# Two down-product operands made in PSUM, and normalization factors kept there, in a one-layer decoder step on Trainium2

## The chip, the cores and the metric

The kernel runs on one core of a Trainium2 chip. The metric is the device time of one execution in microseconds (us): median 1795.73 us of 3 runs, 1795.71 to 1795.86. Five engines work side by side: PE (matmul), DVE (elementwise, VectorE), ACT (activation, copies, casts, ScalarE), POOL (elementwise, GpSimd) and SP, which issues the DMAs. Each runs its own instructions in a fixed order and waits where a value or a buffer is not ready. Matmul results go to PSUM, which this kernel cuts into eight banks. Everything else lies in SBUF.

## What is computed

One layer of a hybrid decoder on 16 meta, 1024 prompt and 32 sample tokens of width 1024, in f32:

```python
x = x + 0.5 * swiglu(rmsnorm(x, g1), w1g, w1u, w1d)
h = rmsnorm(x, gm)
z = h @ w_in + b_in
...
x = x + jnp.concatenate([c, q], axis=-1) @ w_out + b_out
x = x + 0.5 * swiglu(rmsnorm(x, g2), w2g, w2u, w2d)
...
y = xf * lax.rsqrt(jnp.mean(xf * xf, axis=-1, keepdims=True) + EPS)     # rmsnorm, then * g
return (jax.nn.silu(x @ wg) * (x @ wu)) @ wd                            # swiglu
```

The two lines left out make c (gated depthwise convolution) and q (pooling) from z. A last rmsnorm gives the outputs.

## The kernel before

**Tokens and numbers.** The 1072 tokens and 2 of padding are cut into three pieces of 358 columns. Feature tiles of 128 lie on the partitions, tokens on the free axis. Every f32 operand is split into a high part in fp32r and a low remainder (`split`: ACT casts the high part, DVE subtracts it to make the low part, L145), and each product is three matmuls (`mul`, L127). Weights come by DMA (`wraw`), ACT casts the high part `wh` (L144) and POOL subtracts for the low part `wl` (L145).

**The two fast passes.** Each FFN has 22 tiles of width, taken in 11 pairs. The first FFN runs a pass over pieces one and two, the second FFN one over two and three, as a block form with seven products instead of eight (`m1` to `m7`). DVE makes the sums of raw weight blocks (`block_steps`, L556 to L559) and, after the products, the sums in `settle` and `add` (L586). Products m3 to m7 stay in their PSUM banks until these sums are done. The result of a gate block goes through `gate`: ACT writes its silu into an SBUF buffer `cc` (L712 in a group, L684 in a plain pair) and the bank is free. The result of an up block goes through `up`.

**Groups.** Eight of the eleven pairs are joined two by two (`group_sink`, four groups in each pass), so that their down product runs in the seven-product form too (`fast_down`). It needs seven operands made of the hidden blocks: b11, b21, t1 to t4, b22. The second pair of a group makes most of them, for halves i = 1 and then i = 0, in this chain on DVE: the block product (L716) into `cc` for b21 and into its own bank for b22; t2 in the bank of b22 by L707 and L708; t3 by the same two lines into an SBUF buffer `tmp`; and t4 by L732 into `cc`. Each is then split (L144 on ACT, L145 on DVE: `dt4l`, `dt3l`). The operands b11, b21, t2 and part of t3 lie in borrowed tiles: `xb` and `hid0` to `hid2`. A down product takes two banks in turn, and DVE adds it to x (L634). While DVE makes these operands, PE already runs the gate block of the next pair and then the down products.

**Normalizations.** `rms_all` or `rms` squares and sums a piece, `rsqrt` (L187 on) takes the root in small DVE operations and lets PE spread the factor over the partitions of a bank. ACT copies it to SBUF as `nr` (L218). `normed` and `fast_operands` then form x times gain times factor (`scaled`, L266) with `x` and `nr` both in SBUF, and split it. Five normalizations run beside matmuls: h1b, hma (two pieces), h2a, s2 (`fast_operands`) and hmb. Plain passes (`plain_ffn`, L505 to L531) run beside them on PE. The first normalization has code of its own (class `Start`) and already reads its factor from the bank; the last one, of the outputs, calls `rms`. The change touches neither.

**Order.** Matmuls stay in program order. All other instructions are ordered by a tile scheduler that lays out a timeline of its own; it also decides which bank a tile gets. POOL has little but the low parts of weights, in the order of the weights.

Of the kernel before, what the change touches and what calls it, by code (L numbers as in the profile page):

```python
# [12 lines left out]
ALU = mybir.AluOpType  # L13
P = 128

D = 1024
# [15 lines left out]
EPS = 1e-6  # L32
# [53 lines left out]
def trunk(ctx: ExitStack, tc: tile.TileContext, xt, wf1, win, wout, wf2, wpool, vec, eye, sconv, spool,  # L86
          yt, ncp, npp, ncs, nps):
    nc = tc.nc
# [9 lines left out]
    def temp():  # L98
        return const.tile([P, N + PHIST - 1], F32, name="tmp", tag="tmp", bufs=T_BUFS)
# [21 lines left out]
    def accum():  # L121
        return pp.tile([P, 512], F32, name="acc", tag="acc")
# [119 lines left out]
    def rms(piece, out):  # L242
        s = yield from square_sum([X(k, piece) for k in range(KD)])
        yield LAG
        out[piece] = yield from rsqrt(s, 1.0 / D, EPS)
# [21 lines left out]

    def rms_all(pieces, out):

        steps, last = None, None  # L270
        for piece in pieces:
            s = yield from square_sum([X(k, piece) for k in range(KD)])
            if steps is not None:
                out[last] = whole(steps)
            yield LAG
            steps, last = rsqrt(s, 1.0 / D, EPS), piece
            next(steps)
        if steps is not None:
            yield LAG2
            out[last] = whole(steps)  # L280

    def normed(pieces, gain, tiles, out, stats=None):


        st = {} if stats is None else stats
        h, lo = tiles()
        yield from rms_all([piece for piece in pieces if piece not in st], st)
        at, lows = 0, []
        for piece in pieces:
            n = piece[1] - piece[0]  # L290
            for k in range(KD):
                t = accum()[:, :n]
                with tc.issue_after(lows[-2].ins) if len(lows) > 1 else nullcontext():
                    scaled(t, piece, k, gain, st[piece])
                yield
                lows.append(split(h[:, k, at : at + n], lo[:, k, at : at + n], t))
                yield
            at += n
        out["h"] = (h, lo)
# [7 lines left out]
    def fast_operands(pieces, gain, out, stats):  # L307

        st = stats
        p0, p1 = pieces
        n = p0[1] - p0[0]
        ops = out["ops"] = operand_tiles(n)

        def put(name, k, t):
            split(ops[name][0][:, k], ops[name][1][:, k], t)

        for piece in pieces:
            if piece not in st:  # L320
                yield from rms(piece, st)
        sub = nc.vector.tensor_tensor
        for k in range(KH):
            b11, b22, b21 = (temp()[:, :n] for _ in range(3))
            t = accum()[:, :n]
            scaled(b11, p0, k, gain, st[p0])
            scaled(b22, p1, KH + k, gain, st[p1])
            yield
            put("b11", k, b11)
            put("b22", k, b22)  # L330
            yield
            scaled(t, p1, k, gain, st[p1])
            t3 = temp()[:, :n]
            sub(t3, b22, t, ALU.subtract)
            sub(t, t, b11, ALU.subtract)
            yield
            put("t1", k, t)
            put("t3", k, t3)
            scaled(b21, p0, KH + k, gain, st[p0])
            yield  # L340
            sub(t, b22, t, ALU.subtract)
            put("t2", k, t)
            put("b21", k, b21)
            yield
            sub(t, b21, t, ALU.subtract)
            put("t4", k, t)
            yield LAG6
# [298 lines left out]
    def fast_ffn(wsrc, pieces, free, get, hid):  # L646

        n = N  # L650
        pairs, downs = [], {}

        def kept():
            return pools["fast"].tile([P, n], F32, name="cc", tag="cc", bufs=4)

        def own(name, part):
            return [pools["fast"].tile([P, n], F32R, name=f"d{name}{'hl'[part]}{i}", tag=f"d{name}{'hl'[part]}{i}")
                    for i in range(2)]

        def borrowed():  # L660

            t = const.tile([P, KD, n], F32R, name="xb", tag=f"x{free}")
            out = {name: tuple([t[:, 4 * i + 2 * part + j] for j in range(2)] for part in range(2))
                   for i, name in enumerate(("b11", "b21"))}
            out["t2"] = tuple([hidden_tile(i, part) for i in range(2)] for part in range(2))
            out["t3"] = ([hidden_tile(2, part) for part in range(2)], own("t3", 1))
            return out

        def places(p):

            for i in range(2):
                if p < PAIRS - 1:
                    hid[2 * p + i] = tuple(own(("t1", "t4")[i], part) for part in range(2))
                elif i == 0:
                    hid[2 * p + i] = tuple(own("b22", part) for part in range(2))
                else:
                    hid[2 * p + i] = tuple([hidden_tile(j, part) for j in (1, 2)] for part in range(2))

        def plain_sink(p):
            silus = {}  # L680

            def gate(i, c, t):
                silus[i, c] = kept()
                nc.scalar.activation(silus[i, c], t, AF.Silu)  # L684

            def up(i, c, t):
                f = 2 * p + i
                nc.vector.tensor_tensor(t, t, silus[i, c], ALU.mult)
                if f not in hid:
                    places(p)  # L690
                split(hid[f][0][c], hid[f][1][c], t)

            return gate, up

        def group_sink(ops, second):
            silus, hs = {}, {}
            sub = nc.vector.tensor_tensor

            def put(name, i, t):
                if not ops:  # L700
                    ops.update(borrowed())
                if name not in ops:
                    ops[name] = own(name, 0), own(name, 1)
                split(ops[name][0][i], ops[name][1][i], t)

            def less(t, s, name, i):
                sub(t, s, ops[name][0][i], ALU.subtract)  # L707
                sub(t, t, ops[name][1][i], ALU.subtract)  # L708

            def gate(i, c, t):  # L710
                silus[i, c] = kept()
                nc.scalar.activation(silus[i, c], t, AF.Silu)  # L712

            def up(i, c, t):
                h = hs[i, c] = t if c else silus[i, c]
                nc.vector.tensor_tensor(h, t, silus[i, c], ALU.mult)  # L716
                if second:
                    put("b22" if c else "b21", i, h)
                elif c == 0:
                    put("b11", i, h)  # L720
                if (i, 1 - c) not in hs:
                    return
                if not second:
                    sub(hs[i, 1], hs[i, 1], hs[i, 0], ALU.subtract)
                    put("t1", i, hs[i, 1])
                    return
                b21, b22, t3 = hs[i, 0], hs[i, 1], temp()[:, :n]
                less(b22, b22, "t1", i)
                put("t2", i, b22)
                less(t3, b22, "b11", i)  # L730
                put("t3", i, t3)
                sub(b21, b21, b22, ALU.subtract)  # L732
                put("t4", i, b21)

            return gate, up

        for p in range(PAIRS):
            start = p if p in GROUPS else p - 1
            if start in GROUPS:
                if p == start:  # L740
                    ops = {}
                    downs[p + 1] = [fast_down(wsrc, p, j, pieces, ops) for j in range(2)]
                gate, up = group_sink(ops, p != start)
            else:
                gate, up = plain_sink(p)
                downs[p] = down_steps(wsrc, p, pieces, hid)
            pairs.append((fast_pair(wsrc[4 * p], wsrc[4 * p + 1], get, n, gate),
                          fast_pair(wsrc[4 * p + 2], wsrc[4 * p + 3], get, n, up)))
        return pairs, downs, places
# [243 lines left out]
    def whole(gen):  # L993

        while True:
            try:
                next(gen)
            except StopIteration as e:
                return e.value
# [14 lines left out]
    box = {k: {} for k in ("s1", "h1b", "hma", "hmb", "ca", "cb", "h2a", "s2")}  # L1014
# [209 lines left out]
    last, room = {}, {}  # L1224
# [65 lines left out]
    steps = [p for p in plan if p[0] == "step"]  # L1290
# [22 lines left out]
    i = 0  # L1313
    credit = 0.0
    for item in plan:
# [3 lines left out]
        while state["made"] <= min(i + 2, len(steps) - 1):  # L1319
            s = steps[state["made"]]  # L1320
# [96 lines left out]
```

## Time and profile before

| | before |
|---|---|
| median of 3 runs | 1795.73 us (1795.71 to 1795.86) |
| the profiled execution | 1794.0 us |
| its span on the core | 1792.2 us |
| PE busy | 1726.9 us, 96% |
| DVE busy | 1384.0 us, 77% |
| POOL busy | 1146.5 us, 64% |
| ACT busy | 759.7 us, 42% |

The span is the time from the first to the last instruction that the profiler saw; the execution adds 1.8 us around it. Busy shares are averages over stages that differ, so they do not tell where PE waits. The views used below are the table of what PE waited for, the timeline (start, duration, engine, line, operation, and in brackets the idle time before it with what ended it) and the groups of DVE instructions by line and form.

### The profile page before, as it was taken

Reading aid. Unit: us, or ns where it says so; the run is one execution under the profiler, and the core shown is the slowest. Engines: PE = TensorE matmul, PEld = TensorE weight load, DVE = VectorE, ACT = ScalarE, POOL = GpSimd, SP = SyncE. Lnnn points to the kernel's source line nnn. Section 1 sums busy time; section 2 is a strip of 40 time slices with the busy share of each in tenths; the row PEclk is TensorE's granted clock in tenths of the full one; section 3 lists DMA queues with packets and bytes.
Section 4 is the critical chain, followed back from the end, with each engine's and each line's share of the span. In section 5 each row is a group of like instructions: output and inputs, shape, how many; then the busy total and the mean of one; then the engine's idle time right before and its main releaser. Section 6 shows DMA issues by size and latency. Waiting matters only on the chain.

```text
span 1792.2 us, 29876 instructions
## 1 busy us (share of the span) xinstructions
PE 1726.9 (96%) x10486; PEld 1710.3 (95%) x10486; DVE 1384.0 (77%) x2621; ACT 759.7 (42%) x1482; POOL 1146.5 (64%) x894
## 2 busy tenths in 40 slices
PE   7799999999999999999999999999999999999997
PEld 6799999999998999999999998999999999999997
DVE  8869898989657795897235888548588989897965
ACT  6434444444444224434235433455453444444344
POOL 5586666667745337667356657765577676767683
PEclk9899999999999999999999999999999999999998
DMA  6122232223353223443234494444332222222232
GB/s 210 33 82 76 71 104 76 70 81 104 101 115 110 81 67 116 124 134 108 71 100 136 130 137 128 136 125 128 108 110 88 71 83 71 83 71 71 71 101 84
DMA packets 115894, 177.70 MB, mean 99 GB/s; under 512 B 28321, under 2 KB 35745, under 8 KB 115745
## 3 DMA queue, kind: packets, MB, share of 16 engines
q1 hardware_dynamic: 115744, 175.80, 33.4%
q8 instruction: 83, 1.36, 0.3%
q14 instruction: 67, 0.54, 0.1%
HBM read 170.60 MB, written 5.15 MB: 98 GB/s over the span
## 4 chain that ended last, share of the span: by engine, by line
PE 73%; DVE 19%; issue 3%; DMA 2%; ACT 1%; POOL 1%; SPq 0%; DVEq 0%; POOLq 0%; ACTq 0%
PE acc L127 73%; DMA wraw<-in_wf 2%; DVE wraw L558 1%; DVE acc L586 1%; DVE tmp L586 1%; DVE acc L830 1%; DVE wraw L557 1%; DVE tmp L708 1%; DVE acc L266 1%; DVE tmp L266 1%; DVE x L505 1%; POOL wl L145 1%; DVE pr L848 1%; DMA x<-in_xt 0%; DVE cc L716 0%
## 5 line engine op out<-in xcount | busy, mean ns | idle before, releaser
L145 POOL TENSOR_TENSOR wl<-wraw,wh 128x512 fp32r<-128x512 f32 x740 | 992.5, 1353 | 581.1 <-ACT wh L144 539.3
L144 ACT CAST wh<-wraw 128x512 fp32r<-128x512 f32 x740 | 452.9, 621 | 662.7 <-PE acc L127 438.8
L127 PE MATMUL acc<-smt,wh 128*128 128x358 f32 x1024 | 253.0, 328 | 1.8 <-DVE mixl L145 1.8
L830 DVE SCALAR_TENSOR_TENSOR acc<-ub,vecs,acc 128x340 f32<-128x340 f32 (+2 forms) x348 | 183.3, 570 | 2.6
L127 PEld LDWEIGHTS acc<-smt,wh 128*128 128x128 f32 x1024 | 181.8, 190 | 2.5 <-DVE mixl L145 2.1
L127 PE MATMUL acc<-smt,wl 128*128 128x358 f32 x512 | 167.7, 328 | 0.0
L127 PE MATMUL acc<-mixlt,wh 128*128 128x340 f32 x704 | 166.7, 321 | 0.8 <-ACT wh L144 0.8
L505 DVE SCALAR_TENSOR_TENSOR x<-acc,x 128x358 f32<-128x358 f32 (+1 forms) x240 | 119.3, 516 | 35.6 <-PE acc L127 34.9
L634 DVE SCALAR_TENSOR_TENSOR x<-acc,x 128x358 f32<-128x358 f32 x320 | 144.8, 515 | 0.0
L586 DVE TENSOR_TENSOR acc<-tmp,acc 128x358 f32<-128x358 f32 x168 | 85.7, 526 | 49.4 <-PE acc L127 46.1
L127 PEld LDWEIGHTS acc<-mixlt,wh 128*128 128x128 f32 x704 | 122.1, 190 | 1.3 <-ACT wh L144 1.1
L127 PE MATMUL acc<-mixlt,wl 128*128 128x340 f32 x352 | 112.8, 320 | 0.8 <-POOL wl L145 0.8
L145 POOL TENSOR_TENSOR wl<-sx,wh 128x512 fp32r<-128x512 f32 x58 | 85.0, 1465 | 29.8 <-ACT wh L144 28.0
L127 PEld LDWEIGHTS acc<-smt,wl 128*128 128x128 f32 x512 | 97.0, 189 | 0.0
L558 DVE TENSOR_TENSOR wraw<-sx,wraw 128x512 f32<-128x512 f32 x58 | 78.6, 1355 | 13.5 <-POOL wl L145 13.4
L127 PE MATMUL acc<-mixh,wh 128*128 128x356 f32 (+1 forms) x320 | 78.4, 325 | 2.1 <-ACT mixh L144 2.1
L127 PE MATMUL acc<-mixl,wh 128*128 128x356 f32 (+1 forms) x320 | 78.0, 325 | 0.0
L127 PE MATMUL acc<-mixh,wl 128*128 128x356 f32 (+1 forms) x320 | 77.9, 325 | 0.0
L557 DVE TENSOR_TENSOR wraw<-wraw 128x512 f32<-128x512 f32 x58 | 75.8, 1307 | 0.4
L586 DVE TENSOR_TENSOR tmp<-tmp,acc 128x358 f32<-128x358 f32 x126 | 65.3, 518 | 14.0 <-PE acc L127 12.8
L559 DVE TENSOR_TENSOR wraw<-wraw 128x512 f32<-128x512 f32 x58 | 71.6, 1235 | 1.6 <-POOL wl L145 1.5
L127 PE MATMUL acc<-b11h,wh 128*128 128x358 f32 x184 | 62.1, 338 | 10.8 <-ACT wh L144 10.8
(286 smaller groups left out, 4765.8 us busy)
## 6 DMA issues: line engine op xcount, KB each, us to landing
wraw<-in_wf SPq DMA_DIRECT2D x544, 256.0 KB, 2.9
wraw<-in_win SPq DMA_DIRECT2D x48, 256.0 KB, 2.9
wraw<-in_wout SPq DMA_DIRECT2D x32, 256.0 KB, 2.9
x<-in_xt SPq DMA_DIRECT2D x8, 179.0 KB, 4.5
tmp<-in_xt SPq DMA_DIRECT2D x8, 179.0 KB, 2.8
x<-in_xt SPq DMA_DIRECT2D x1, 1432.0 KB, 7.3
x<-in_xt SPq DMA_DIRECT2D x8, 178.0 KB, 4.4
out_yt<-tmp SPq DMA_DIRECT2D x8, 170.0 KB, 3.3
```

The costliest lines, as they stand in the source:

```text
L127: tc.keep_in_program_order(nc.tensor.matmul(acc, lhs, rhs, start=start, stop=stop))
L144: nc.scalar.copy(hi, src)
L145: return (engine or nc.vector).tensor_tensor(lo, src, hi, ALU.subtract)
L266: nc.vector.scalar_tensor_tensor(t, X(k, piece), col(gain, k), r, ALU.mult, ALU.mult)
L505: nc.vector.scalar_tensor_tensor(X(m, piece), acc, 0.5, X(m, piece), ALU.mult, ALU.add)
L557: nc.vector.tensor_tensor(a21, a11, a21, ALU.subtract)
L558: nc.vector.tensor_tensor(a11, s1, a11, ALU.subtract)
L559: nc.vector.tensor_tensor(a12, a12, a11, ALU.subtract)
L586: nc.vector.tensor_tensor(t, s, acc, ALU.add)
L634: nc.vector.scalar_tensor_tensor(to, acc, 0.5 * sign, to, ALU.mult, ALU.add)
L708: sub(t, t, ops[name][1][i], ALU.subtract)
L830: nc.vector.scalar_tensor_tensor(to, src, w, part, ALU.mult, ALU.add)
```

## The change

Two edits. In a group's second pair, t4 is now made before t3. t3 is made in place in the bank of b22. For i = 1 the product b21 also stays in its bank, ACT copies it to SBUF as an operand, and t4 is made in the bank; for i = 0 it stays in `cc`. In the five normalizations the factors stay in their banks (`box["psum"]`) while `scaled` runs over all tiles; factors that are already known in SBUF (one for h1b, one for s2) are copied by ACT into a bank.

```diff
     def rms_all(pieces, out):
...
+        def done(piece, box):
+            whole(steps)
+            out[piece] = box["psum"]
...
             if steps is not None:
-                out[last] = whole(steps)
+                done(*last)
             yield LAG
-            steps, last = rsqrt(s, 1.0 / D, EPS), piece
+            box = {}
+            steps, last = rsqrt(s, 1.0 / D, EPS, box, False), (piece, box)
             next(steps)
...
+    def in_banks(pieces, st):
+
+        known = [piece for piece in pieces if piece in st]
+        yield from rms_all([piece for piece in pieces if piece not in st], st)
+        for piece in known:
+            r = accum()[:, : piece[1] - piece[0]]
+            nc.scalar.copy(r, st[piece])
+            st[piece] = r
+        yield
...
-        yield from rms_all([piece for piece in pieces if piece not in st], st)
+        yield from in_banks(pieces, st)
...
-        for piece in pieces:
-            if piece not in st:
-                yield from rms(piece, st)
+        yield from in_banks(pieces, st)
...
             def up(i, c, t):
-                h = hs[i, c] = t if c else silus[i, c]
+                h = hs[i, c] = t if c or (second and i) else silus[i, c]
...
-                b21, b22, t3 = hs[i, 0], hs[i, 1], temp()[:, :n]
-                less(b22, b22, "t1", i)
-                put("t2", i, b22)
-                less(t3, b22, "b11", i)
-                put("t3", i, t3)
-                sub(b21, b21, b22, ALU.subtract)
+                b21, t = hs[i, 0], hs[i, 1]
+                if i:
+                    t4 = temp()[:, :n]
+                    nc.scalar.copy(t4, b21)
+                less(t, t, "t1", i)
+                put("t2", i, t)
+                sub(b21, t4 if i else b21, t, ALU.subtract)
                 put("t4", i, b21)
+                less(t, t, "b11", i)
+                put("t3", i, t)
```

PE's order is the same as before, and so is POOL's but for one place in the sample tokens' part. What moves stands on DVE. The names carry the tile's number here; lines of the changed kernel are 15 or 16 higher (L707 is L722, L708 is L723, L732 is L748, L586 is L601). This is DVE at the end of the third group of the first pass (315 to 335 us of the trace), for half i = 0, before:

```order
L707 TENSOR_TENSOR tmp_3540<-acc_3523,xb_3075 128x358
L732 TENSOR_TENSOR cc_3243<-cc_3243,acc_3523 128x358
L586 TENSOR_TENSOR acc_3571<-tmp_3569,acc_3571 128x358
L559 TENSOR_TENSOR wraw_3465<-wraw_3465,wraw_3339 128x512
L557 TENSOR_TENSOR wraw_3647<-wraw_3512,wraw_3647 128x512
L708 TENSOR_TENSOR tmp_3540<-tmp_3540,xb_3075 128x358
L586 TENSOR_TENSOR tmp_3569<-tmp_3569,acc_3591 128x358
L145 TENSOR_TENSOR dt4l0_3506<-cc_3243,dt4h0_3504 128x358
L586 TENSOR_TENSOR tmp_3622<-tmp_3569,acc_3608 128x358
L145 TENSOR_TENSOR dt3l0_3082<-tmp_3540,hid2h_3080 128x358
L586 TENSOR_TENSOR tmp_3569<-tmp_3569,acc_3628 128x358
L586 TENSOR_TENSOR acc_3628<-tmp_3622,acc_3628 128x358
```

The t3 chain of before is L707 and L708 on `tmp_3540` and the low part `dt3l0`. The add into `acc_3628`, the last row, makes the block from which ACT takes the first silu. The same place after:

```order
L748 TENSOR_TENSOR cc_3243<-cc_3243,acc_3524 128x358
L722 TENSOR_TENSOR acc_3524<-acc_3524,xb_3075 128x358
L601 TENSOR_TENSOR tmp_3622<-tmp_3569,acc_3608 128x358
L574 TENSOR_TENSOR wraw_3465<-wraw_3465,wraw_3339 128x512
L572 TENSOR_TENSOR wraw_3647<-wraw_3513,wraw_3647 128x512
L723 TENSOR_TENSOR acc_3524<-acc_3524,xb_3075 128x358
L145 TENSOR_TENSOR dt4l0_3503<-cc_3243,dt4h0_3501 128x358
L601 TENSOR_TENSOR tmp_3569<-tmp_3569,acc_3628 128x358
L601 TENSOR_TENSOR acc_3628<-tmp_3622,acc_3628 128x358
L601 TENSOR_TENSOR acc_3657<-tmp_3622,acc_3657 128x358
L145 TENSOR_TENSOR dt3l0_3082<-acc_3524,hid2h_3080 128x358
L601 TENSOR_TENSOR acc_3686<-tmp_3569,acc_3686 128x358
```

The t3 chain now works in `acc_3524`, `dt3l0` stands behind two of the three adds into banks, and two adds (the one into `acc_3571` and the one that reads `acc_3591`) have moved ahead of this stretch. In `fast_operands` (DVE, beside the plain pass, 1259 to 1264 us of the trace) the order was:

```order
L266 SCALAR_TENSOR_TENSOR acc_14358<-x2_4993,vecs_63,nr_13897 128x358
L531 TENSOR_TENSOR acc_14281<-acc_14281,tmp_14267 128x340
L334 TENSOR_TENSOR tmp_14366<-tmp_14356,acc_14358 128x358
L335 TENSOR_TENSOR acc_14358<-acc_14358,tmp_14355 128x358
L266 SCALAR_TENSOR_TENSOR tmp_14357<-x1_62,vecs_63,nr_13501 128x358
L505 SCALAR_TENSOR_TENSOR x0_61<-acc_14323,x0_61 128x340
```

and is now, in the same order, with the factor read from a bank (`acc_13887`, `acc_13891`) instead of `nr`:

```order
L266 SCALAR_TENSOR_TENSOR acc_14352<-x2_4993,vecs_63,acc_13887 128x358
L546 TENSOR_TENSOR acc_14275<-acc_14275,tmp_14261 128x340
L349 TENSOR_TENSOR tmp_14360<-tmp_14350,acc_14352 128x358
L350 TENSOR_TENSOR acc_14352<-acc_14352,tmp_14349 128x358
L266 SCALAR_TENSOR_TENSOR tmp_14351<-x1_62,vecs_63,acc_13891 128x358
L520 SCALAR_TENSOR_TENSOR x0_61<-acc_14317,x0_61 128x340
```

Only operands moved here. SP issues three of the loads of the early sum of squares (`early_rms`, in the second group) a few places earlier than before.

## Rows read from the trace of the kernel before

**Rows 1.** The page: span, and busy time of each engine.

```profile
span 1792.2 us, 29876 instructions
...
PE 1726.9 (96%) x10486; PEld 1710.3 (95%) x10486; DVE 1384.0 (77%) x2621; ACT 759.7 (42%) x1482; POOL 1146.5 (64%) x894
```

**Rows 2.** What PE waited for: us in total, times, longest us.

```profile
PE acc L127 <- DVE diag L209: 14.0, 4, 7.5
...
PE acc L127 <- ACT cc L712: 5.8, 6, 1.2
PE acc L127 <- DVE x L505: 5.0, 4, 2.7
...
PE acc L127 <- ACT cc L684: 2.5, 2, 1.2
...
PE acc L127 <- DVE tmp L586: 1.3, 1, 1.3
...
PE acc L127 <- DVE x L634: 0.7, 2, 0.5
```

**Rows 3.** Timeline, third group, all engines: start, us, engine, line, idle before.

```profile
327.94 0.68 DVE L557 TENSOR_TENSOR wraw<-wraw 128x512 f32<-128x512 f32 x1
...
328.10 1.68 POOL L145 TENSOR_TENSOR wl<-wraw,wh 128x512 fp32r<-128x512 f32 x1 [0.96 <-PE acc L127]
...
328.54 1.62 DVE L708 TENSOR_TENSOR tmp<-tmp,xb 128x358 f32<-128x358 f32 x1
...
330.52 1.20 DVE L145 TENSOR_TENSOR dt4l<-cc,dt4h 128x358 fp32r<-128x358 f32 x1
...
332.08 1.18 DVE L145 TENSOR_TENSOR dt3l<-tmp,hid2h 128x358 fp32r<-128x358 f32 x1
...
332.21 0.43 PE L127 MATMUL acc<-hid0h,wh 128*128 128x358 f32 x1
...
333.61 1.40 DVE L586 TENSOR_TENSOR acc<-tmp,acc 128x358 f32<-128x358 f32 x3
334.17 0.97 ACT L712 ACTIVATE cc<-acc 128x358 f32<-128x358 f32 x2 [2.96 <-DVE acc L586]
...
334.69 0.43 PE L127 MATMUL acc<-hid0h,wh 128*128 128x358 f32 x1 [1.24 <-ACT cc L712]
```

**Rows 4.** Timeline of PE: two normalizations and the last group.

```profile
574.36 0.43 PE L127 MATMUL acc<-hid2h,wh 128*128 128x358 f32 x1 [1.40 <-DVE x L505]
...
1263.63 0.42 PE L127 MATMUL acc<-hid2h,wh 128*128 128x340 f32 x1 [2.71 <-DVE x L505]
...
1679.99 0.43 PE L127 MATMUL acc<-hid0h,wh 128*128 128x358 f32 x1 [1.23 <-ACT cc L684]
```

**Rows 5.** Timeline of DVE: the products with the factor in those two normalizations.

```profile
571.30 2.13 DVE L266 SCALAR_TENSOR_TENSOR acc<-x,vecs,nr 128x356 f32<-128x356 f32 x2
...
1256.42 2.08 DVE L266 SCALAR_TENSOR_TENSOR tmp<-x,vecs,nr 128x358 f32<-128x358 f32 x2
...
1259.74 1.62 DVE L266 SCALAR_TENSOR_TENSOR acc<-x,vecs,nr 128x358 f32<-128x358 f32 x1
```

**Rows 6.** Groups of DVE instructions by form: count, busy us, mean ns.

```profile
L557 DVE TENSOR_TENSOR wraw<-wraw 128x512 f32<-128x512 f32 x58 | 75.8, 1307 | 0.4
...
L266 DVE SCALAR_TENSOR_TENSOR acc<-x,vecs,nr 128x358 f32<-128x358 f32 x28 | 22.7, 820 | 0.6 <-ACT nr L218 0.6
L708 DVE TENSOR_TENSOR tmp<-tmp,xb 128x358 f32<-128x358 f32 x16 | 22.3, 1394 | 0.0
...
L145 DVE TENSOR_TENSOR dt3l<-tmp,hid2h 128x358 fp32r<-128x358 f32 x8 | 8.8, 1094 | 0.0
...
L708 DVE TENSOR_TENSOR acc<-acc,dt1l 128x358 f32<-128x358 f32 x16 | 8.5, 528 | 0.0
...
L266 DVE SCALAR_TENSOR_TENSOR acc<-x,vecs,acc 128x358 f32<-128x358 f32 x8 | 4.6, 585 | 0.0
...
L145 DVE TENSOR_TENSOR dt3l<-tmp,hid2l 128x358 fp32r<-128x358 f32 x8 | 4.2, 519 | 0.0
```

More of the change, by code (lines that the diff above doesn't have):

```diff
@@ L279, in rms_all @@
             yield LAG2
-            out[last] = whole(steps)
+            done(*last)
+    def in_banks(pieces, st):
[6 more added lines that the diff above has]
+        yield
     def normed(pieces, gain, tiles, out, stats=None):
```

## The prediction, made before the changed kernel ran

> **What bounds the kernel now.** PE is busy for 1726.9 of 1792.2 us [rows 1], so a change that leaves PE's order alone can win only from the 65.3 us in which PE stands still. I read the table of PE's waits first, then the timeline at the largest of them, then the groups of DVE instructions there. The largest entry, 14.0 us behind `diag`, is for the most part the first normalization, which the change does not touch [rows 2]. The entries in reach are those put down to a silu (`cc`, L712 and L684: 8.3 us in eight waits), to L505 (5.0 us in four), and to L586 and L634 (1.3 and 0.7 us) [rows 2].
>
> The silu waits repeat one pattern: about 1.23 us in each of six group ends, of which the first (start 334.69) and the last (1679.99) are shown [rows 3, 4]. At 332.21 PE begins a down product, and the next, at 334.69, waits 1.24 us for a bank that a silu frees. ACT is not late by itself: it stood idle for 2.96 us until an add of L586 was done. DVE had no gap there, and three of its instructions took long: L708 into `tmp` 1.62 us, `dt4l` 1.20, `dt3l` 1.18, each while POOL made the low part of a weight (the first beside the one that starts at 328.10) [rows 3]. By form, L708 with both inputs in SBUF takes 1394 ns in the mean, and with one in a bank 528; the same subtraction of `dt3l` takes 1094 ns for i = 0 and 519 for i = 1 [rows 6]. So these instructions are long because of what else runs, not because of their size. L266 shows it too: 820 ns with the factor in SBUF, 585 with it in a bank [rows 6].
>
> **The groups.** On DVE the change shortens L708 for i = 0 from 1.62 to 0.53 us, 1.09 less, and takes `dt3l`, 1.18 us, from ahead of the add that releases the first silu to behind it [rows 3]; there it should cost 0.5. For i = 1 L708 falls from 1.39 in the mean to 0.53, 0.8 less after rounding down [rows 6]; `dt4l` of i = 1 now reads a bank too and can only shorten, which I leave out. Together 3.1 us before the first silu. The two adds that moved forward only fill what this opens, so I count nothing for them.
>
> The need has moved too. In the changed kernel as built, t3 of i = 0 keeps its bank until `dt3l`, so the scheduler gives the first down product (332.21) the bank of the first silu and the second (334.69 now, 333.45 without its wait) the bank of `dt3l`. Before, the silu that PE waited for ended at about 334.64, which is when PE went on. Less 3.1 it ends at 331.5, 0.7 us ahead of its new need. `dt3l` would end two adds and itself later, 331.1 + 0.9 + 0.5 = 332.5, 0.9 ahead of 333.45. Where both hold, all 1.23 us go. What is late next is whatever DVE still does with two inputs in SBUF: L557 ran for 0.68 us here but takes 1307 ns in the mean [rows 3, 6], so it, its neighbour L559 or `dt4l` may meet POOL at the new phase, each for 0.6 us more, and two of these use up the margin. I take 1.0 of 1.23 for each of six: **6.0 us** (ends 0 and 7.4).
>
> The other two groups of the first pass and two waits for L634 and L586 make up the rest: 0.9 of the silu waits (8.3 less 7.4), 1.3 and 0.7, together 2.9 [rows 2]. The second group also carries the early sum of squares, whose ACT and DVE work waits for loads, and SP's earlier issue of three of these costs nothing that PE sees, since the weights ahead in that queue are already fetched in advance; if it did delay a weight, it would be by one load. I take **2.1** in all (ends 0 and 2.9). Besides, PE has waits too short to be marked in these views, and those in group ends should shrink with DVE's queue: **1.0**, a choice (0 to 2).
>
> Eight copies of b21 come to ACT and five copies of factors go, two come. A silu takes 0.47 us there; at that price eight are 3.8 us, hidden by idle time such as the 2.96 us [rows 3]. A new wait stands in it: the copy waits for L716, and behind it in ACT's queue are casts of weights and silus; DVE's t4 then waits for the copy. It lies in the half i = 1, before the stretch shown, and DVE has other work between. Without that cover it is 0.5 us a group, 4 us in all.
>
> **The normalizations.** At 574.36 PE waited 1.40 us and at 1263.63 2.71 us for a bank that L505 frees [rows 4], and L505 stood behind L266 in DVE's order. Two of L266 at 571.30 took 2.13 us; at 0.58 each they take 1.1, 1.0 less, and earlier ones in the same run shrink as well. At 1256.42 two took 2.08, 1.0 less, and the one at 1259.74 1.62, 1.04 less; the upstream ones of the same normalization add more [rows 5]. So both waits go: 4.1 us. Two smaller ones of the same entry, 5.0 − 4.1 = 0.9 us, go by about half: 0.4. Sum **4.5** (ends 2.0 and 5.0). The rest of the 820 ns rows are in normalizations where PE waits for nothing, so their gain lies off the path.
>
> **What it costs.** Factors now hold a bank each while L266 runs over eight tiles, two of eight in `hma` and `fast_operands`. PE's plain pass there needs one bank for each product, and DVE clears them faster. I take 1.0 us of new waits, between none and 4 (four waits of the 1.0 us that a contended L266 costs).
>
> One rule speaks against the change. The groups' path has three instructions for i = 0 that leave SBUF for a bank. The subtraction of `dt3l` from SBUF takes 519 ns and one within a bank 528, 9 more [rows 6], and I cost the move at nothing. The Trainium skill, page "Perfetto Trace Analysis", section "Optimizing Scalar/DVE Operations", gives DVE an overhead of about 60 ns on SBUF and 125 on PSUM for each instruction. By it, an estimate, three times 65 ns in six groups would take 1.2 us off the gain.
>
> **Sum.** 6.0 + 2.1 + 1.0 + 4.5 − 1.0 = 12.6 us. The profiled execution of 1794.0 us would take 1781.4. It lies 1.7 below the median of the runs, and the same gain on the median gives **1783.1**. With all the upper ends and no new waits, 7.4 + 2.9 + 2 + 5.0, the gain is 17.3 and the time 1778.4; with 4 us of the groups' gain lost it is 1787.1.
>
> **Rivals.** *A, the collision only moves.* POOL's chain of low parts has the same order, and DVE still has L556 to L559 and `dt4l` with two inputs in SBUF. If shorter DVE work only lets these start into POOL's instructions, two of them at 0.6 and one at 0.7 take 1.9 of 3.1 us back, the first silu ends at 333.4, PE waits 1.2 at the first down product instead of the second, and the groups gain nothing. For it: L557's mean of 1307 against 0.68 here [rows 3, 6]. Against it: L708 and `dt3l` are collisions that no longer can happen. Normalizations alone: 4.5 + 1.0 − 1.0 = 4.5 with something of the rest: 1790.5.
>
> *B, banks run short; slower.* A bank is now held by t3 until `dt3l` and by t4 of i = 1 until `dt4l`, and the first down product depends on a silu for which it had no need before. The point that decides is the end of that silu: PE's wait is this end less 332.21, and it passes the old 1.24 us once the silu ends after 333.45, that is when less than 1.2 of the 3.1 us arrive. With none arriving, the wait is 2.43 instead of 1.24, 1.2 more in each of eight group ends, 9.6 us; less 4.5 from normalizations, 5.1 slower: 1800.8. For it: PE's waits there are for banks. Against it: rows 3 show where 2.3 of the 3.1 us come from. (The Trainium skill, "Perfetto Trace Analysis", section "Optimization Strategy", takes the same gap repeating on the engine that should be saturated as a sign that there may be too little SBUF or PSUM; the six waits of about 1.23 us look like that, and by that rule a change that holds banks longer makes them worse.)
>
> *C, the gain is off the path.* DVE is freed, but PE waits as long for something else that ends at the same time, such as POOL's low parts or DMA: 1795. Against it: in neither place do rows show PE held by POOL.
>
> *D, more comes.* The short waits all go and later stretches follow: 1776.
>
> **How the numbers follow.** Forecast 0.67 (1778 to 1788), A 0.18, B 0.05, C 0.06, D 0.04. About 0.2% (3.6 us) is what a measurement of this kernel can tell from no change: faster means under 1792.1. A counts as faster for 0.14 and as same for 0.04. So faster 0.85, same 0.10, slower 0.05. The range leaves out B, C, a third of A and half of D: 1777 to 1791.5.
>
> **What would show it.** In the changed trace the six waits for a silu should be gone or under 0.4 us, L708 and `dt3l` should all be near 0.53 us and L266 near 0.58, the waits at about 574 and 1263 gone. Waits at the first down product of a group end would show A or B; A if L556 to L559 or `dt4l` there are long, B if they are not. I would be wrong in the large if new waits appear where two factors hold banks, beside the plain passes.

## The result

The changed kernel takes 1774.74 us, median of 4 runs (1772.80 to 1776.07), against 1795.72 before on the same comparison: ratio 0.9885, 95% interval 0.9873 to 0.9897. That is 21 us faster. The direction was forecast and the size was not: 1783.1 with a range from 1777.0, so the time lies 2.3 us below the range and the gain is 1.7 times the 12.6 forecast. Of the rivals D, "more comes" (1776, given 0.04), lies nearest in time.

The profiled execution took 1772.8 us (1794.0 before). On the page, span and busy times, to set beside [rows 1]:

```profile
span 1771.0 us, 29845 instructions
...
PE 1719.3 (97%) x10486; PEld 1708.7 (96%) x10486; DVE 1359.0 (77%) x2621; ACT 761.8 (43%) x1487; POOL 1141.0 (64%) x894
```

The span is 21.2 us shorter. DVE is busy for 25 us less. PE runs the same matmuls in the same order and still shows 7.6 us less busy time. So the waits marked on its matmuls, which the forecast added up, cannot hold the whole gain: some of the lost time was counted as busy, and some of it passed at a lower clock (below).

What PE waited for (total, times, longest, in us), beside [rows 2]; lines of the changed kernel are 15 higher around the groups:

```profile
PE acc L127 <- DVE diag L209: 14.0, 4, 7.5
...
PE acc L127 <- ACT cc L727: 1.7, 1, 1.7
...
PE acc L127 <- DVE hid2l L145: 1.4, 1, 1.4
...
PE acc L127 <- DVE smt L145: 0.5, 1, 0.5
PE acc L127 <- DVE x L520: 0.2, 1, 0.2
```

The eight silu waits (8.3 us before) are one of 1.7, and L520, which was L505, fell from 5.0 to 0.2. `smt` is new, 0.5 us: it is in h1b. `hid2l` (0.6 before) stands at 1089 us, where nothing was edited.

The end of the third group, all engines (start, duration, engine, line, idle before), beside [rows 3]:

```profile
325.00 1.61 DVE L574 TENSOR_TENSOR wraw<-wraw 128x512 f32<-128x512 f32 x1
...
326.53 1.79 DVE L572 TENSOR_TENSOR wraw<-wraw 128x512 f32<-128x512 f32 x1
...
328.25 0.53 DVE L723 TENSOR_TENSOR acc<-acc,xb 128x358 f32<-128x358 f32 x1
...
328.69 0.52 DVE L145 TENSOR_TENSOR dt4l<-cc,dt4h 128x358 fp32r<-128x358 f32 x1
...
329.56 0.96 DVE L601 TENSOR_TENSOR acc<-tmp,acc 128x358 f32<-128x358 f32 x2
...
330.12 0.91 ACT L727 ACTIVATE cc<-acc 128x358 f32<-128x358 f32 x2 [0.34 <-DVE acc L601]
...
330.44 0.52 DVE L145 TENSOR_TENSOR dt3l<-acc,hid2h 128x358 fp32r<-128x358 f32 x1
330.65 0.19 PEld L127 LDWEIGHTS acc<-hid0h,wh 128*128 128x128 f32 x1 [0.21 <-ACT cc L727]
330.65 0.43 PE L127 MATMUL acc<-hid0h,wh 128*128 128x358 f32 x1
```

L708, now L723, takes 0.53 us instead of 1.62, `dt4l` 0.52 instead of 1.20, and `dt3l` 0.52 and it stands behind the first two adds into banks. But the two sums of raw weights, L574 and L572 (0.68 each before), now take 1.61 and 1.79. The first silu starts at 330.12, and PE's weight load at 330.65 still waited 0.21 us for it: no margin is left.

By form (count, busy us, mean ns), beside [rows 6]:

```profile
L572 DVE TENSOR_TENSOR wraw<-wraw 128x512 f32<-128x512 f32 x58 | 87.6, 1511 | 0.4
...
L266 DVE SCALAR_TENSOR_TENSOR acc<-x,vecs,acc 128x358 f32<-128x358 f32 x36 | 21.0, 590 | 0.3 <-PE acc L127 0.2
...
L723 DVE TENSOR_TENSOR acc<-acc,xb 128x358 f32<-128x358 f32 x16 | 8.4, 527 | 0.0
...
L145 DVE TENSOR_TENSOR dt3l<-acc,hid2h 128x358 fp32r<-128x358 f32 x8 | 4.1, 518 | 0.0
L145 DVE TENSOR_TENSOR dt4l<-cc,dt4h 128x358 fp32r<-128x358 f32 x8 | 4.1, 518 | 0.0
```

Everything that was moved into a bank takes 518 to 590 ns, as the rows with a bank operand said. L572, with both inputs in SBUF and not touched, rose from 1307 to 1511 ns: a part of the collisions moved there.

### The profile page after: what moved, and what is told of

It reads as the page before. It is cut to its first block, busy times and chain, and to the rows that moved or that the text cites. A ratio compares the mean times of both kernels' runs of the same rounds, so it can differ in the third digit from the quotient of the medians.

```text
span 1771.0 us, 29845 instructions
## 1 busy us (share of the span) xinstructions
PE 1719.3 (97%) x10486; PEld 1708.7 (96%) x10486; DVE 1359.0 (77%) x2621; ACT 761.8 (43%) x1487; POOL 1141.0 (64%) x894
## 4 chain that ended last, share of the span: by engine, by line
PE 65%; DVE 5%; DMA 1%; issue 1%; ACT 0%; POOL 0%; DVEq 0%; ACTq 0%; POOLq 0%
PE acc L127 65%; DMA wraw<-in_wf 1%; DVE acc L848 1%; DVE pr L866 1%; DVE x L520 0%; DVE cb L868 0%; POOL wl L145 0%; DVE acc L238 0%; DVE acc L917 0%; DVE acc L546 0%; ACT wh L144 0%; DVE acc L266 0%; DVE diag L209 0%; DVE acc L601 0%; DVE acc L703 0%
## 5 line engine op out<-in xcount | busy, mean ns | idle before, releaser
L520 DVE SCALAR_TENSOR_TENSOR x<-acc,x 128x358 f32<-128x358 f32 (+1 forms) x240 | 119.9, 518 | 36.8 <-PE acc L127 36.1
L601 DVE TENSOR_TENSOR acc<-tmp,acc 128x358 f32<-128x358 f32 x168 | 86.3, 526 | 49.3 <-PE acc L127 46.0
L572 DVE TENSOR_TENSOR wraw<-wraw 128x512 f32<-128x512 f32 x58 | 87.6, 1511 | 0.4
L573 DVE TENSOR_TENSOR wraw<-sx,wraw 128x512 f32<-128x512 f32 x58 | 74.5, 1285 | 12.7 <-POOL wl L145 12.6
L574 DVE TENSOR_TENSOR wraw<-wraw 128x512 f32<-128x512 f32 x58 | 77.9, 1343 | 1.6 <-POOL wl L145 1.5
L601 DVE TENSOR_TENSOR tmp<-tmp,acc 128x358 f32<-128x358 f32 x126 | 65.3, 519 | 14.3 <-PE acc L127 13.3
```

The lines of the kernel that those rows point to most:

```text
L520: nc.vector.scalar_tensor_tensor(X(m, piece), acc, 0.5, X(m, piece), ALU.mult, ALU.add)
L572: nc.vector.tensor_tensor(a21, a11, a21, ALU.subtract)
L573: nc.vector.tensor_tensor(a11, s1, a11, ALU.subtract)
L574: nc.vector.tensor_tensor(a12, a12, a11, ALU.subtract)
L601: nc.vector.tensor_tensor(t, s, acc, ALU.add)
```

## The experiments

Each kernel was compared with the kernel before on the same chip. "Shifts" below are differences of start times of the same PE instruction in two traces, added up over a stretch. The medians:

| kernel | median us | before, us | ratio (95% interval) |
|---|---|---|---|
| changed kernel, again | 1773.80 | 1796.36 | 0.9873 (0.9856 to 0.9889) |
| groups alone | 1781.18 | 1795.71 | 0.9924 (0.9908 to 0.9941) |
| norms alone | 1790.01 | 1795.71 | 0.9968 (0.9958 to 0.9978) |
| t3 alone | 1780.36 | 1795.71 | 0.9923 (0.9900 to 0.9946) |
| order alone | 1799.88 | 1795.71 | 1.0031 (1.0017 to 1.0044) |
| norms, banks held, factor in SBUF | 1799.74 | 1797.36 | 1.0013 (1.0003 to 1.0022) |
| t4 in PSUM for both halves | 1781.05 | 1796.36 | 0.9915 (0.9900 to 0.9930) |
| changed, without the t4 part | 1778.14 | 1797.36 | 0.9888 (0.9873 to 0.9903) |
| changed, h1b's factor in SBUF | 1777.10 | 1797.36 | 0.9882 (0.9867 to 0.9897) |
| both of these | 1775.33 | 1796.36 | 0.9880 (0.9865 to 0.9895) |

**The two halves apart.** Theory 1: the mechanism is the forecast one, and the group ends were mis-sized. Rival, theory 2: the groups gave what was forecast and the surplus has another source. Groups alone is the kernel before with the new `up`; norms alone the kernel before with `in_banks` and `box["psum"]`.

> Only the edit of the groups (t3 and, for i = 1, t4 made in PSUM); the factors of the normalizations go to SBUF as before. Theory 1 (the group ends gave more than forecast, because a pause of PE is longer than the idle time marked on its matmul): the shifts of PE's starts between the two traces add up to 13.5 us in the eight group ends, so about 1782.2 against 1795.7. Theory 2 (the groups gave what was forecast, 9.1 us, and the rest came from elsewhere): about 1786.6.

> Only the factors of the normalizations kept in PSUM; the groups as before. Theory 1: the shifts of PE's starts at the normalizations add up to 5.5 us with a loss of 0.6 at h1b in it, so about 1790.2. Theory 2: the normalizations and what follows them gave the surplus, 10 us or more, 1786 or less. If both parts alone add up to about 19 us and the whole gave 21, some 2 us lie outside both or in how they act together.

Measured: 14.5 us and 5.7 us faster. The groups exceed theory 2 by 5 us, and the norms stay far below it. By the shifts the group ends give 13.0 us in groups alone and 13.8 in the changed kernel, and the norms 5.5 in both, so the halves hardly act on each other. The medians (20.2 us against 21.0) do not show that by themselves, since each half also contains the 2 us at 820 us that are taken up below. Theory 1 stands.

**What in the groups does it.**

```diff
-                b21, b22, t3 = hs[i, 0], hs[i, 1], temp()[:, :n]
-                less(b22, b22, "t1", i)
-                put("t2", i, b22)
-                less(t3, b22, "b11", i)
-                put("t3", i, t3)
-                sub(b21, b21, b22, ALU.subtract)
+                b21, t = hs[i, 0], hs[i, 1]
+                less(t, t, "t1", i)
+                put("t2", i, t)
+                sub(b21, b21, t, ALU.subtract)
                 put("t4", i, b21)
+                less(t, t, "b11", i)
+                put("t3", i, t)
```

> Of the groups' edit only t3: made in place in the bank of b22, after t4; t4 is made in SBUF for both halves, no copy on ACT, factors as before. If the collisions of the t3 chain with POOL make the waits: nearly all of the groups' gain, 10 to 13 us, 1783 to 1786. If the t4 part is needed to bring the silu in time: about half, 1789.

```diff
-                less(t3, b22, "b11", i)
-                put("t3", i, t3)
                 sub(b21, b21, b22, ALU.subtract)
                 put("t4", i, b21)
+                less(t3, b22, "b11", i)
+                put("t3", i, t3)
```

> Only the order: t4 before t3, with t3 still made in an SBUF buffer. If collisions are the cause: no change, 1794 to 1797, L708 still at 1.4 us and six waits for a silu of about 1.23 us. If the order is the cause: 8 us or more faster.

t3 alone gave 15.4 us (10 to 18 by the interval), as much as the whole edit of the groups. The order alone made the kernel 4.2 us slower, which neither theory had expected; by the shifts it loses 6.5 us in the six group ends, against which stand the 2 us at 820 us that it gains like the others (below). The two kernels differ only in where t3 is made and lie 19.5 us apart. In the order-only trace the chain still collides, a little more than before (columns as above):

```profile
L708 DVE TENSOR_TENSOR tmp<-tmp,xb 128x358 f32<-128x358 f32 x16 | 24.5, 1529 | 0.0
...
L145 DVE TENSOR_TENSOR dt3l<-tmp,hid2h 128x358 fp32r<-128x358 f32 x8 | 10.1, 1262 | 0.0
```

Its weight loads on PE (total, times, longest, in us) wait for the silus as before and for L586 besides:

```profile
PEld acc L127 <- DVE tmp L586: 11.1, 8, 1.6
...
PEld acc L127 <- issue: 7.6, 5, 3.2
PEld acc L127 <- ACT cc L712: 7.4, 6, 1.4
```

Before, that entry of L586 was 3.4 us (below). The banks that the adds to `tmp` free come later, for two reasons: `dt4l` (0.5 us) now stands ahead of these adds, and earlier L557 meets POOL and takes 1.1 us more than in [rows 3]:

```profile
329.27 1.78 DVE L557 TENSOR_TENSOR wraw<-wraw 128x512 f32<-128x512 f32 x1
```

PE now stops earlier in the down product and again for the silu. So making t3 in the bank is what wins, and the new order by itself costs.

That POOL is the reason for the long instructions can be read from the trace of the kernel before, one instruction at a time. The L708 into `tmp`, `dt4l` from `cc` and `dt3l` from `tmp`, all with both inputs in SBUF, stand there 48 times. The 29 that start while POOL is in a low part take 1.17 to 1.62 us, and each ends 0.39 us after POOL's instruction ends. The other 19 take 0.52, also the 8 beside which POOL starts later. At the third group, after the POOL row at 328.10 in [rows 3], which ends at 329.78, come

```profile
329.73 1.60 POOL L145 TENSOR_TENSOR wl<-sx,wh 128x512 fp32r<-128x512 f32 x1
331.30 1.57 POOL L145 TENSOR_TENSOR wl<-wraw,wh 128x512 fp32r<-128x512 f32 x1
```

and L708, `dt4l` and `dt3l` end at 330.16, 331.72 and 333.26. In the changed kernel L723 and `dt3l` take 0.52 to 0.53 us beside POOL too. No run took POOL's work away.

**Is it the bank or the port in the norms?** The factor occupies its bank, held by a copy of one column at the end, and L266 reads `nr`:

```diff
-            steps, last = rsqrt(s, 1.0 / D, EPS, box, False), (piece, box)
+            steps, last = rsqrt(s, 1.0 / D, EPS, box, True), (piece, box)
...
-            st[piece] = r
+            held.append(r)
...
+    def release(held):
+        for r in held:
+            nc.scalar.copy(const.tile([P, 1], F32, name="hold", tag="hold"), r[:, :1])
```

> Norms alone, groups as before: every factor occupies its bank as in the changed kernel (a copy of one column at the end holds it), but L266 reads the factor from SBUF as before; seven copies of one column and seven of a factor are added on ACT. If the gain of the norms (1790.0 us with the factors read in PSUM, against 1795.7) comes from L266 reading a bank: no gain or a loss, 1795 to 1800, with L266 at about 0.8 us and the waits near 574 and 1263 as before or longer. If it comes from the new order of the code alone: about 1790.

No gain, 0.1% slower. L266 is as slow as before (count, busy us, mean ns):

```profile
L266 DVE SCALAR_TENSOR_TENSOR acc<-x,vecs,nr 128x358 f32<-128x358 f32 x28 | 23.8, 859 | 0.7 <-ACT nr L218 0.6
```

and of L505's waits (5.0 us before; its line is L528 here) 3.7 stay, the one of 2.7 among them:

```profile
PE acc L127 <- DVE x L528: 3.7, 4, 2.7
```

Between 1235 and 1264 us the changed kernel gains 4.5 us by the shifts and this one nothing, so there the gain comes from L266 reading the factor in a bank. At 574 us this is not shown: the wait of 1.40 us goes in this run too (1.2 us by the shifts) with L266 as slow as before. PE waits there 0.27 us for `mixl` instead, as if the product had another bank; what ended the wait stays open.

**Is there room for more?** The t4 of i = 0 is made in PSUM too:

```diff
-                h = hs[i, c] = t if c or (second and i) else silus[i, c]
+                h = hs[i, c] = t if c or second else silus[i, c]
...
-                if i:
-                    t4 = temp()[:, :n]
-                    nc.scalar.copy(t4, b21)
+                t4 = temp()[:, :n]
+                nc.scalar.copy(t4, b21)
...
-                sub(b21, t4 if i else b21, t, ALU.subtract)
+                sub(b21, t4, t, ALU.subtract)
```

> The changed kernel with t4 made in PSUM for i = 0 too, with a copy on ACT and one bank more held at each group end. Rival B (banks are short): a wait of 1 us or more comes back at most of the eight group ends, 8 us slower than the changed kernel. If banks are not short: within 1.5 us of it.

It is 7.3 us slower than the changed kernel, where rival B said 8. PE waits at the down product for a bank that `dt4l` frees, in the table and at the third group:

```profile
PE acc L127 <- DVE dt4l L145: 4.9, 6, 0.8
```

```profile
330.12 0.59 PE L127 MATMUL acc<-xb,wh 128*128 128x358 f32 x2 [0.81 <-DVE dt4l L145]
```

So rival B is real, one bank further on: with the instructions in this order the eight banks are just enough for the change as it was made.

**What the rest is worth.** The changed kernel without the t4 part, with h1b's factor in SBUF (`normed` calls `rms_all` as before), and with both:

> The changed kernel without the t4 part: t3 in PSUM, t4 in SBUF for both halves and no copy on ACT, all factors in PSUM. If t4 in PSUM for i = 1 adds nothing: equal to the changed kernel (1773.8 to 1774.7) within 1 us. If it gives something: 1 us or more slower.

> The changed kernel, with the known factor of h1b read from SBUF as before and thus one bank less held there. If the wait at 487 us (0.51 us marked, 0.63 to 0.67 by PE's starts) is the price of that bank: it goes, and the kernel is 0.6 us faster, about what a comparison can just tell. If L266 with both inputs in SBUF delays PE there: no faster or slower.

> t3 in PSUM, t4 in SBUF for both halves, factors in PSUM but for h1b, whose known factor is read from SBUF as before. If the t4 part gives nothing and the bank held in h1b costs the 0.67 us that the traces show at 489 to 494: 0.7 to 1.5 us less than the changed kernel. If t4 in PSUM gives something when both edits are in: slower than the changed kernel by 1 us or more.

All three lie in each other's intervals and in that of the changed kernel; none can be told from it. The wait in h1b does go in the trace when the bank is not held (0.63 us by the shifts, as expected), which is too little for a comparison. The t4 part and its copies on ACT gave nothing that could be measured. None beats the changed kernel.

**What repeats.** The two kernels once more, for second traces (before: one run, 1798.47 us):

> The kernel before once more, for a second trace. Against the first trace of before, every other kernel's trace gains about 2.1 us at 817 to 829 us and 2 us at 1063 to 1075 us, also those that change nothing there. Theory 1 (these belong to one execution): the waits in these two stretches differ here from those of the first trace by a microsecond or more, and the silu waits (1.23 us, six times), 574 (1.40) and 1263 (2.71) repeat within 0.05 us. Theory 2 (the change does something there): all of them repeat.

> The changed kernel beside the other versions on one chip: 1774.7 us, 1773 to 1776.5.

The silu waits and the norms' waits of before repeat within 0.05 us. So does the wait at 820 us, which theory 1 had put down to chance: it belongs to the kernel before. The stretch at 1063 to 1075 us differs between executions of one kernel (0.5 us here) and by up to 5 between the changed versions. No edit explains it, but it is part of the total (below).

## Why the prediction was too small, step by step

**The silu waits: right place, mis-sized.** The forecast took 1.23 us for each of six group ends as a ceiling and 1.0 as the value, 6.0 in all. By the shifts these ends gave 1.59, 1.61, 1.59, 1.61, 1.58 and 1.61, together 9.6. Of the 3.6 us too little, 1.4 are the discount from 1.23 to 1.0 and 2.2 lie above what was marked. The idle time that is marked on a matmul is not what PE loses. Before, at the third group (start, duration):

```profile
328.09 0.50 PE L127 MATMUL acc<-xb,wh 128*128 128x358 f32 x2
...
332.97 0.33 PE L127 MATMUL acc<-hid1l,wh 128*128 128x358 f32 x1
333.14 0.32 PE L127 MATMUL acc<-hid1h,wl 128*128 128x358 f32 x1
...
335.78 0.33 PE L127 MATMUL acc<-hid2h,wh 128*128 128x358 f32 x1
```

and after:

```profile
326.62 0.50 PE L127 MATMUL acc<-xb,wh 128*128 128x358 f32 x2
...
332.74 0.32 PE L127 MATMUL acc<-hid2h,wh 128*128 128x358 f32 x1
```

From the first `xb` to the first `hid2h` it is 7.69 us and 6.12: 1.57 gained where 1.24 was marked. The matmul at 333.14 is shown to end 0.32 us later, at 333.46, and the wait is counted from there; but without a pause matmuls start every 0.17 us (332.97, 333.14), so PE could have started the next one at 333.3. And there was a second, unmarked pause before 332.21. PE's weight loads show both, in the kernel before:

```profile
332.21 0.19 PEld L127 LDWEIGHTS acc<-hid0h,wh 128*128 128x128 f32 x1 [0.31 <-DVE tmp L586]
...
334.69 0.19 PEld L127 LDWEIGHTS acc<-hid0h,wh 128*128 128x128 f32 x1 [1.53 <-ACT cc L712]
...
345.86 0.30 PEld L127 LDWEIGHTS acc<-xb,wh 128*128 128x128 f32 x2 [0.36 <-issue]
```

0.31 and 1.53 are 1.84 us, and after the change 0.21 is left (330.65, above): 1.63 gained.

**"Short waits", 1.0: the size within its range, the cause wrong.** The row at 345.86 shows a pause of 0.36 us put down to "issue", some 10 us after the group end. Before, it stands behind most group ends, and it goes. By the shifts five such places gave 0.30, 0.33, 0.32, 0.33 and 0.45, 1.7 us. I had thought that it would shrink with DVE's queue; but it goes in the order-only kernel too, where DVE's queue is longer, and stays in norms alone. It depends on the groups' code. What PE waits for there stays open.

The totals of PE's weight loads (total, times, longest, in us), before:

```profile
PEld acc L127 <- issue: 9.1, 9, 3.2
PEld acc L127 <- ACT cc L712: 7.5, 6, 1.5
PEld acc L127 <- DVE x L505: 6.3, 5, 3.0
...
PEld acc L127 <- DVE tmp L586: 3.4, 7, 1.6
PEld acc L127 <- ACT cc L684: 3.0, 2, 1.5
```

and after:

```profile
PEld acc L127 <- issue: 6.6, 4, 3.2
...
PEld acc L127 <- ACT cc L727: 3.1, 6, 2.0
...
PEld acc L127 <- DVE x L520: 0.5, 1, 0.5
PEld acc L127 <- ACT cc L699: 0.4, 2, 0.2
```

These five entries fall from 29.3 to 10.6 us, 18.7 of the 21.2. On the matmuls the forecast saw 8.3 + 1.3 for silus and L586; here they are 13.9.

**The other two groups, 2.1: close.** 0.79 at 162 us, 0.44 around 247, 0.50 at 259 and 0.75 at 1521, 2.5. The second group of the first pass kept a wait for a silu (1.7 us at 245 us): L572 takes 1.81 us ahead of the adds that release it. In the second trace it takes 0.68 and two waits of 0.6 us are left.

**The margin of 0.7 us: wrong, though the marked wait went.** Of the 3.1 us 2.6 arrived: counted from the first `xb` of the down product the first silu ended after 6.55 us before (334.17 + 0.47 − 328.09) and after 3.96 now (330.12 + 0.46 − 326.62). L574 and L572 lost 2.0 us in collisions, which is rival A's mechanism; `dt4l`, for which I counted nothing, gave back 0.7 and the two adds moved ahead 0.9. One more collision, and a marked wait would have stayed. Both traces of the changed kernel show these ends alike, so it was not the luck of one execution.

**The norms: 4.5 less 1.0 forecast, 5.5 measured.** The two waits gave 1.66 at 574 us and 2.98 at 1263, with 1.40 and 2.71 marked: the same undercount, about 0.26 each. The smaller ones in `fast_operands` gave 1.5 instead of 0.4, since the whole run of L266 there is shorter. The cost of held banks was 0.64 us, in h1b alone, instead of 1.0.

**Costs taken as nothing.** The copies on ACT showed no wait, as forecast. `dt3l` took 519 ns from SBUF without a collision and 518 from a bank. So the rule that weighed against the change, an overhead of about 60 ns for DVE on SBUF and 125 on PSUM (the Trainium skill, "Perfetto Trace Analysis", "Optimizing Scalar/DVE Operations"), does not show here. The sum was right to leave the 1.2 us out.

**Not forecast at all: a wait at 820 us, and where PE's clock falls.** No instruction that the change edits runs at 817 to 829 us. The kernel before waited 1.77 us at the first matmul of a plain pass, the changed one 1.22 (PE, start, duration, idle before):

```profile
820.64 0.59 PE L127 MATMUL acc<-smt,wh 128*128 128x358 f32 x2 [1.77 <-DVE mixl L145]
```

```profile
813.73 0.57 PE L127 MATMUL acc<-smt,wh 128*128 128x358 f32 x2 [1.22 <-ACT wh L144]
```

Before, PE waits for a bank that `mixl` (DVE, in the mixer's background work) frees last; after, only for the cast of the weights. This points to another bank for the product, chosen by the scheduler; no view here shows the bank itself. That is 0.55 us. The rest of the 2.0 us that the shifts show at this place is PE's clock. Windows before (us, PE, PEld, DVE, ACT, POOL busy, PE's clock, DMA share, GB/s):

```profile
core 0: us, PE busy (x) PEld busy (x) DVE busy (x) ACT busy (x) POOL busy (x), PEclk, DMA share, GB/s
822.00:825.20 3.20, 3.20 (x12) 3.20 (x12) 3.20 (x6) 0.70 (x2) 2.07 (x2) 0.50 0.28 84
```

and after, behind the same wait and some 37 us later:

```profile
814.00:817.00 3.00, 3.00 (x20) 3.00 (x19) 2.96 (x8) 0.18 (x1) 2.92 (x4) 1.00 0.04 16
851.40:854.80 3.40, 3.25 (x11) 3.18 (x12) 2.47 (x5) 2.35 (x6) 0.00 (x0) 0.51 0.22 77
```

Before, PE's granted clock was 0.50, that is 1.2 GHz instead of 2.4, for the 3.2 us from 822; after, it stayed at 1.00 there. But the slow stretch did not go away for good. Both kernels wait equally long at a later matmul, before and after:

```profile
859.85 0.43 PE L127 MATMUL acc<-mixh,wh 128*128 128x358 f32 x1 [2.06 <-ACT mixh L144]
```

```profile
851.55 0.67 PE L127 MATMUL acc<-mixh,wh 128*128 128x358 f32 x1 [2.06 <-ACT mixh L144]
```

Behind this wait the clock was 1.00 before and 0.51 after, and the changed kernel loses 1.2 us there by the shifts (1.5 in its second trace). So most of what the clock gave at 822 us was paid back at 851.

Both traces of before show the longer wait and the slow clock at 822; every other version but one has the shorter wait and the full clock there, order-only among them, and most of them have the slow clock at the second wait instead. So nearly any edit of the code that re-ran the scheduler changed this wait: a side effect of the change, not of its idea. The one exception, the norms with banks held, kept the wait (1.76 us) and yet its clock stayed at 1.00, so the length of the pause alone does not set the clock; what does stays open.

Two more places differ without an edit. At 1055 to 1080 us the changed kernel is 2.5 us faster in both its traces: it lacks one wait of 0.80 us for the cast of a weight, and the half clock that stands in both traces of before from about 1068 us on for 3.4 us. At 1090 to 1115 it is 1.0 us slower.

**The sum.** Group ends and what follows them 9.6 + 2.5 + 1.7 = 13.8 (forecast 9.1), norms 5.5 (3.5): 19.3 of 21.2 us. The other 1.9 us are a balance that was not forecast: 2.0 at 820 us, −1.2 at 851, 2.5 at 1055 to 1080, −1.0 at 1090 to 1115 and −0.4 elsewhere, most of it in the first 130 us. That they leave no more is chance. Without them the gain would still lie beyond the forecast's upper end of 17.3. So the mechanism held, and the step that failed is the size of its two main terms: the pauses were read off the idle time marked on the matmuls, the group ends were discounted for a late silu besides, and the smaller waits of the norms were taken at half.

## What to carry to other kernels

Where PE is the bound, price a pause by the distance between starts of two matmuls that straddle it, or by the weight loads' rows, and not by the idle time marked on the matmul; here six waits marked 1.23 us were worth 1.6. Elementwise work of DVE that has both inputs in SBUF and starts while POOL makes a low part took 1.2 to 1.6 us here instead of 0.5, until 0.39 us after POOL was done; an operand that is in PSUM already should stay there as long as a bank is free, and one bank further the gain turns into waits for banks. Any edit re-runs the scheduler, so look at waits for banks and at the clock far from the edit too: here they moved 1 to 2.5 us at single places, in both directions.

## What the runs showed of the hardware

Not expected: after a pause of 1.77 us PE ran 3.2 us at half its clock in both traces of the kernel before, and after one of 1.76 us at the same place in another version it did not, so a pause that looks the same can cost 1.6 us more or less (the shifts between these two over the stretch). The same holds for the pause of 2.06 us: half the clock behind it in the changed kernel, full clock in the kernel before. At most group ends of before, PE's weight loads stood still for about 0.35 us with nothing shown that they wait for; it follows the groups' code and not the load on the other engines. In the trace of before, an instruction of DVE with both inputs in SBUF that started while POOL was in an instruction ended a fixed time after POOL's: 0.39 us for L708, `dt4l` and `dt3l` (29 of 29), 0.37 to 0.40 for L266 reading `nr` (25 of 25, 340 to 358 columns), 0.55 for the sums of raw weights in L557 and L559 (92 of 93). And a collision can move rather than vanish: one sum of raw weights, untouched, rose from 1307 to 1511 ns in the mean when the t3 chain left SBUF.
